# Stick-breaking attention on one core: the strict mask as an additive operand of the running product's scan

## The chip, the cores and the metric

The kernel runs on one core of a Trainium2 chip. The time is the device time of one execution in microseconds (us), taken as the median of several executions. The engines are TensorE (PE for matmuls, PEld for weight loads), VectorE (DVE), ScalarE (ACT), GpSimd (POOL) and SyncE (SP), which issues the DMAs.

## The reference, cut to what matters

Two layers, each a token mixer with two attention branches and a squared-ReLU MLP, over 1024 tokens of width 1024, in float32. The change touches the stick-breaking branch (8 heads of 64), of which this is the core:

```python
z = jnp.einsum('bqhd,bshd->bhqs', qb, kb).astype(jnp.float32) * scale
...
strict = s_idx < t_idx
log_keep = jnp.where(strict, -jax.nn.softplus(z), 0.0)
tail = lax.cumsum(log_keep, axis=3, reverse=True) - log_keep
w = jnp.where(strict, jnp.exp(jax.nn.log_sigmoid(z) + tail), 0.0)
outs.append(jnp.einsum('bhqs,bshd->bqhd', w.astype(v.dtype), vb))
```

In words: query t gives key s < t the weight sigmoid(z_ts) times the product of sigmoid(-z_tj) over all keys j between s and t, and no weight to keys s >= t.

## The kernel before

The whole program is one instruction stream per engine, written out by a planner at build time. Each piece of work is a Python generator (a process) that names the engine it wants and an estimated cost; the planner grants each engine to the waiting process of the lowest rank and emits its instructions in that order. On the chip each engine then runs its own list in order and waits where an operand is not there yet. So a changed cost or wait in one process can shift the order of others around it.

A layer has these stages: RMSNorm with transposes (L436), projections, sliding-window attention, stick-breaking attention (`sb_phase`), the merge of both branches under gates, the output projection, and the MLP. Float32 products are made of three matmuls on split operands (`three`, L346 to L348). The gate projections (`gates`, tiles `hT` and `wh` or `wl`, 512 columns wide) have the lowest priority and fill PE wherever a stage leaves it free; five of the sixteen gate blocks start late in `sb_phase` and end after it.

Inside `sb_phase`, each head is cut into four chunks `ci` of two query tiles `tt` (128 queries each). For a query tile the keys 0 to 128(tt+1) are taken in segments of at most 512 columns that start at `c0`: one segment for tt < 4, two (`c0` = 512, then `c0` = 0) for tt >= 4. That makes 12 segments for a head, and 192 for 8 heads and two layers. `weights` handles one of them:

- PE: two matmuls form the scores `z` (L979, L980). In the segment that holds the diagonal (c1 == n, 128 of the 192) a third matmul (L982) adds `sb_mask`, a bf16 tile that is 0 below the diagonal and -1e30 on and above it, with the bf16 identity `ident_b` as weights.
- ACT: `keep` = sigmoid(-z) (L988) and `cc` = sigmoid(z) (L991). The four `keep` tiles are 513 columns wide; column 512 holds 1.0.
- DVE: a scan over `keep[:, lo+1:513]` from right to left multiplies up the running product in place (L999, with `lo` = 512 - m for m columns). A lower segment (`c0` = 0 of two) starts its scan from `carry`, which the upper one made with one 128x1 multiplication (L1003). Then `cc` is multiplied by the products (L1006).
- POOL: a lower segment's column 512 is set back to 1.0 (L1009) and the `keep` tile is free.

Then `chunk` transposes the weights on PE (L1050, fp32, with the identity), ACT and DVE split them into `th` and `tl` (L1056, L1058), and PE multiplies them by the values `vall` (L1082, L1083). The result `o` (L1088, L1090) goes to the scratch `o_sb` (L1093), which the merge loads again (L322). `a_slots` (4) hands out the `keep` tiles, `c_slots` (7) the `cc` tiles, and `Bank("z")` four of the eight PSUM banks.

Of the kernel before, what the change touches and what calls it, by code (L numbers as in the profile page):

```python
# [9 lines left out]
F32 = mybir.dt.float32  # L10
F32R = mybir.dt.float32r
BF16 = mybir.dt.bfloat16
AF = mybir.ActivationFunctionType
ALU = mybir.AluOpType
AX = mybir.AxisListType

P = 128
T = 1024
D = 1024
# [5 lines left out]
NEG = -1e30  # L25
# [36 lines left out]
def f32(ap):  # L62
    return ap.bitcast(F32)
# [135 lines left out]
def tile_hybrid_trunk(ctx: ExitStack, tc: tile.TileContext, x, g_mix, g_mlp, g_rope, sinks, rope,  # L199
                      w_swa, w_qk, w_v, w_gate, w_br, w_out, w_up, w_down, out):  # L200
    nc = tc.nc
# [5 lines left out]
    def act_set(name):  # L207

        if tables_[0] != name:
            tables_[0] = name  # L210
            nc.scalar.preload_act_table_set(name)
# [4 lines left out]
    def pool(name, side="left", space=None):  # L216
        kw = {} if space is None else {"space": space}
        if space is None:
            kw["side"] = side
            kw["reuse_waits"] = "tile"  # L220
        return tc.alloc_tile_pool(name=name, bufs=1, **kw)
# [3 lines left out]
    cp = pool("const")  # L225
# [1 line left out]
    tp = pool("acts")  # L227
    gp = pool("stage")

    ident = cp.tile([P, P], F32, name="ident")  # L230
    make_identity(nc, ident)
    ident_r = cp.tile([P, P], F32R, name="ident_r")
    nc.vector.tensor_copy(ident_r, ident)
    ident_b = cp.tile([P, P], BF16, name="ident_b")
    nc.vector.tensor_copy(ident_b, ident)
    sb_mask = cp.tile([P, P], BF16, name="sb_mask")
    nc.gpsimd.memset(sb_mask, 0.0)
    nc.gpsimd.affine_select(out=sb_mask, in_=sb_mask, compare_op=ALU.is_gt, fill=NEG, base=0,
                            pattern=[[-1, P]], channel_multiplier=1)
    win_mask = cp.tile([P, 256], F32, name="win_mask")  # L240
    nc.gpsimd.memset(win_mask, 0.0)
    prev, cur = win_mask[:, 0:P], win_mask[:, P:256]
    nc.gpsimd.affine_select(out=prev, in_=prev, compare_op=ALU.is_gt, fill=-NEG, base=0,
                            pattern=[[1, P]], channel_multiplier=-1)
    nc.gpsimd.affine_select(out=cur, in_=cur, compare_op=ALU.is_ge, fill=-NEG, base=0,
                            pattern=[[-1, P]], channel_multiplier=1)
# [5 lines left out]
    def act(n):  # L252
        return n * .00083 + .095

    def dve(n):
        return n * .00104 + .068
# [4 lines left out]
    def scan(n):  # L261
        return n * .00225 + .04

    def mm(n):
        return max(n, 256) * .000417 + .0133
# [589 lines left out]


    def sb_phase(l, base, start, opened, q_opened, hT, o_scr, finished, late):
        sb, vall = None, None

        def open_pool():  # L860
            nonlocal sb, vall
            yield opened
            sb = pool("sb")
            vall = sb.tile([P, NT, SBH, 2, HD], F32R, name="vall")
            sb_pool[:] = [sb]
            for i in range(4):
                keeps.append(sb.tile([P, 513], F32, name=f"keep{i}"))
                nc.gpsimd.memset(keeps[i][:, 512:513], 1.0)
            ready.set(sb)

        ready = Event(plan)
        keeps = []
        plan.spawn(open_pool(), base)
        v_ev = [[Event(plan) for _ in range(NT)] for _ in range(2)]
        qk_ev = [Event(plan, 2) for _ in range(SBH)]
        qk_slots = Slots(plan, 2)
        a_slots, c_slots, t_slots, o_slots = Slots(plan, 4), Slots(plan, 7), Slots(plan, 3), Slots(plan, 2)
# [87 lines left out]
        def weights(h, tt, c0, carry_in, carry_out, z_done, got):  # L965
            n = P * (tt + 1)
            c1 = min(n, c0 + 512)
            m = c1 - c0
            yield ready
            yield qk_ev[h]  # L970
            qs, k1, k2 = qk_ev[h].value
            yield a_slots
            yield c_slots
            b = Bank("z")
            yield from b.take()
            yield "P", 2 * max(mm(m) if m > 128 else .11, .11) + (.06 if c1 == n else 0)
            z = b.tile()[:, :m]
            qt = qs[:, tt * P:(tt + 1) * P]
            nc.tensor.matmul(z, qt, k1[:, c0:c1], start=True, stop=False)  # L979
            nc.tensor.matmul(z, qt, k2[:, c0:c1], start=False, stop=c1 != n)  # L980
            if c1 == n:
                nc.tensor.matmul(z[:, m - P:m], ident_b, sb_mask, start=False, stop=True)  # L982
            z_done.done()

            keep, lo = keeps.pop(), 512 - m
            yield "A", act(m)
            act_set(SIGMOID)
            nc.scalar.activation(keep[:, lo:512], z, AF.Sigmoid, scale=-1.0)  # L988
            yield "A", act(m)
            cc = sb.tile([P, 512], F32, tag="c", name="c", bufs=7)[:, :m]  # L990
            nc.scalar.activation(cc, z, AF.Sigmoid)  # L991
            b.free()
            ini = 1.0
            if carry_in:
                yield carry_in
                ini = carry_in.value
            yield "D", scan(m)
            later = keep[:, lo + 1:513]
            nc.vector.tensor_tensor_scan(later[:, ::-1], later[:, ::-1], later[:, ::-1], ini, ALU.mult, ALU.bypass)  # L999
            if carry_out:  # L1000
                yield "D", .12
                carry = sb.tile([P, 1], F32, tag="carry", name="carry", bufs=6)
                nc.vector.tensor_tensor(carry, later[:, 0:1], keep[:, lo:lo + 1], ALU.mult)  # L1003
                carry_out.set(carry)
            yield "D", dve(m)
            nc.vector.tensor_tensor(cc, cc, later, ALU.mult)  # L1006
            if carry_in:
                yield "G", .1
                nc.gpsimd.memset(keep[:, 512:513], 1.0)  # L1009
            keeps.append(keep)  # L1010
            a_slots.release()
            got.set(cc)

        last_av = [None]
# [1 line left out]
        def chunk(h, ci, z_done):  # L1016
# [3 lines left out]
            for i, c0 in enumerate(starts):  # L1020
                for tt in (2 * ci, 2 * ci + 1):
                    got = Event(plan)
                    seg[tt, c0] = got
                    two = len(starts) == 2
                    got.carry = Event(plan) if two and c0 else None
                    cin = seg[tt, 512].carry if two and not c0 else None
                    plan.spawn(weights(h, tt, c0, cin, got.carry, z_done, got), rank + i * 2 + (tt % 2))
# [869 lines left out]
    def driver():  # L1897
# [4 lines left out]
        for l in range(depth):  # L1902
# [37 lines left out]
            plan.spawn(swap_right(swp, projected, q_opened), base)  # L1940
            swa_phase(l, base, sw, swp, hT, normed, o_swa, tab_scr, done, sb_on, projected)
            sb_phase(l, base, sb_on, opened, q_opened, hT, o_sb, sb_done, sb_late)
            yield done
            sw.release()
# [158 lines left out]
```

## Time and profile before

| | |
|---|---|
| median of 3 executions | 2726.43 us (2725.91 to 2731.25) |
| the profiled execution's own time | 2727.98 us |
| its span from the first instruction to the last | 2726.2 us |
| PE busy | 2691.2 us, 99% of the span |
| DVE, ACT, POOL busy | 1904.0, 1402.4, 8.9 us |
| mean granted TensorE clock | 0.996 of full speed |

The profile is of one execution, which lies 1.55 us above the median. A PE that is busy all the time isn't one at its fastest: matmuls overlap, so what one costs is read from the distance between its start and the start of the next, not from its duration.

### The profile page before, as it was taken

The page shows a single profiled execution, that of the slowest core. Times are in us where ns is not written, and L with a number is a line of the kernel's source. Part 1 is how long each engine was busy: PE and PEld are TensorE (multiplying, and loading weights), DVE is VectorE, ACT ScalarE, POOL GpSimd, SP SyncE. Part 2 cuts the span into 40 slices and gives each one's busy share as a digit, 9 for nine tenths or more (in the row PEclk, how much of TensorE's full clock was granted, in tenths as well). Part 3 has the DMA queues.
Part 4 walks back from the last instruction along what each step waited for, and adds up shares of the span by engine and source line. Part 5 has one row for each costly group of instructions (what it writes and reads, how often), then busy time and mean ns, then how long its engine had stood idle before and what let it go on. Part 6 is the DMA issues. An engine that isn't in the chain of part 4 may idle for free.

```text
span 2726.2 us, 37142 instructions
## 1 busy us (share of the span) xinstructions
PE 2691.2 (99%) x13568; PEld 2280.9 (84%) x13568; DVE 1904.0 (70%) x3269; ACT 1402.4 (51%) x2777; POOL 8.9 (0%) x83
## 2 busy tenths in 40 slices
PE   7999999999999999999999999999999999999999
PEld 7888888888878888888888988888888788888887
DVE  6665888855597777767766657887646877768664
ACT  5775556643365445333457766565424644553332
POOL 0000000000000000000000000000000000000000
PEclk9999999999999999999999999999999999999999
DMA  4222221164034447996433222123530444489972
GB/s 169 82 91 71 62 62 56 52 229 164 31 120 161 142 165 265 350 375 246 160 123 94 65 63 66 58 58 97 213 147 31 147 138 160 151 318 354 339 265 88
DMA packets 159382, 411.00 MB, mean 151 GB/s; under 512 B 18656, under 2 KB 32992, under 8 KB 159200
## 3 DMA queue, kind: packets, MB, share of 16 engines
q1 hardware_dynamic: 159200, 408.63, 42.9%
q8 instruction: 107, 1.75, 0.2%
q14 instruction: 75, 0.61, 0.1%
HBM read 285.88 MB, written 114.29 MB: 147 GB/s over the span
## 4 chain that ended last, share of the span: by engine, by line
PE 95%; DVE 2%; ACT 1%; DMA 1%; issue 0%; SPq 0%; DVEq 0%; ACTq 0%
PE bank L346 28%; PE bank L347 28%; PE bank L348 27%; PE bank L1050 2%; PE bank L1083 1%; PE bank L979 1%; PE bank L980 1%; PE bank L1082 1%; PE bank L694 1%; PE bank L436 1%; PE bank L761 1%; PE bank L784 0%; PE bank L783 0%; PE bank L668 0%; PE bank L982 0%
## 5 line engine op out<-in xcount | busy, mean ns | idle before, releaser
L1266 ACT CAST operand<-dr 128x1024 fp32r<-128x1024 f32 x224 | 220.3, 1048 | 348.8 <-PE bank L348 179.1
L347 PE MATMUL bank<-operand 128*128 128x512 f32 x896 | 348.8, 389 | 0.5 <-DVE operand L1269 0.5
L346 PE MATMUL bank<-operand 128*128 128x512 f32 x896 | 348.9, 389 | 0.0
L1269 DVE TENSOR_TENSOR operand<-dr,operand 128x1024 fp32r<-128x1024 f32 x224 | 262.7, 1222 | 123.3 <-ACT operand L1266 123.0
L348 PE MATMUL bank<-operand 128*128 128x512 f32 x896 | 348.6, 389 | 0.0
L346 PE MATMUL bank<-hT,wh 128*128 128x512 f32 (+1 forms) x776 | 312.3, 402 | 0.0
L348 PE MATMUL bank<-hT,wl 128*128 128x512 f32 (+1 forms) x776 | 302.8, 390 | 0.0
L347 PE MATMUL bank<-hT,wh 128*128 128x512 f32 (+1 forms) x776 | 302.4, 390 | 0.0
L347 PEld LDWEIGHTS bank<-operand 128*128 128x128 f32 x896 | 168.2, 188 | 36.2 <-DVE operand L1269 1.4
L348 PEld LDWEIGHTS bank<-operand 128*128 128x128 f32 x896 | 168.2, 188 | 34.9
L346 PEld LDWEIGHTS bank<-operand 128*128 128x128 f32 x896 | 168.2, 188 | 34.8
L1266 ACT CAST wh<-raw 128x512 fp32r<-128x512 f32 x128 | 78.6, 614 | 187.4 <-DVE raw L1280 127.3
L348 PEld LDWEIGHTS bank<-hT,wl 128*128 128x128 f32 x776 | 146.5, 189 | 31.6
L347 PEld LDWEIGHTS bank<-hT,wh 128*128 128x128 f32 x776 | 147.2, 190 | 23.7 <-DVE hT L395 0.2
L346 PEld LDWEIGHTS bank<-hT,wh 128*128 128x128 f32 x776 | 147.3, 190 | 23.3
L332 ACT CAST wh<-raw 128x1024 fp32r<-128x1024 f32 x88 | 92.4, 1051 | 102.6 <-PE bank L348 76.6
L335 DVE TENSOR_TENSOR wl<-raw,wh 128x1024 fp32r<-128x1024 f32 x88 | 107.1, 1219 | 53.4 <-ACT wh L332 52.5
L999 DVE TENSOR_TENSOR_SCAN keep<-keep 128x128 f32<-128x128 f32 (+3 forms) x128 | 100.1, 809 | 16.2 <-ACT keep L988 16.2
L988 ACT ACTIVATE keep<-bank 128x128 f32<-128x128 f32 (+1 forms) x192 | 91.3, 499 | 38.7 <-PE bank L982 23.1
L1058 DVE TENSOR_TENSOR tl<-bank,th 128x512 fp32r<-128x512 f32 (+1 forms) x160 | 97.5, 626 | 18.2 <-ACT th L1056 16.6
L1056 ACT CAST th<-bank 128x512 fp32r<-128x512 f32 (+1 forms) x160 | 83.3, 546 | 49.2 <-PE bank L1050 46.1
L1280 DVE TENSOR_TENSOR dr<-dr 128x1024 f32<-128x1024 f32 x64 | 78.1, 1224 | 40.7 <-DMA dr<-t_scr 16.2
(201 smaller groups left out, 6592.8 us busy)
## 6 DMA issues: line engine op xcount, KB each, us to landing
dr<-in_w_down_dram SPq DMA_DIRECT2D x144, 512.0 KB, 7.7
dr<-u_scr SPq DMA_DIRECT2D x112, 512.0 KB, 6.9
u_scr<-up SPq DMA_DIRECT2D x160, 256.0 KB, 2.8
raw<-in_w_up_dram SPq DMA_DIRECT2D x68, 512.0 KB, 3.5
raw<-in_w_gate_dram SPq DMA_DIRECT2D x32, 512.0 KB, 4.2
g_scr<-stage SPq DMA_DIRECT2D x64, 256.0 KB, 2.4
gate<-g_scr SPq DMA_DIRECT2D x64, 256.0 KB, 3.0
u_scr<-stage SPq DMA_DIRECT2D x64, 256.0 KB, 4.0
```

The lines of the kernel that those rows point to most:

```text
L332: nc.scalar.copy(hi[:, :n], raw[:, :n])
L335: nc.vector.tensor_tensor(lo[:, :n], raw[:, :n], f32(hi[:, :n]), ALU.subtract)
L346: nc.tensor.matmul(ps_ap, ah, bh, start=first, stop=False)
L347: nc.tensor.matmul(ps_ap, ah, bl, start=False, stop=False)
L348: nc.tensor.matmul(ps_ap, al, bh, start=False, stop=last)
L988: nc.scalar.activation(keep[:, lo:512], z, AF.Sigmoid, scale=-1.0)
L999: nc.vector.tensor_tensor_scan(later[:, ::-1], later[:, ::-1], later[:, ::-1], ini, ALU.mult, ALU.bypass)
L1056: nc.scalar.copy(th[:, :n], tr[:, :n])
L1058: nc.vector.tensor_tensor(tl[:, :n], tr[:, :n], f32(th[:, :n]), ALU.subtract)
L1266: nc.scalar.copy(op.hi(j, n), src)
L1269: nc.vector.tensor_tensor(op.lo(j, n), src, f32(op.hi(j, n)), ALU.subtract)
L1280: nc.vector.tensor_tensor(out, a, b, op)
```

## The change

The mask matmul, its bf16 identity and the mask tile go. The scan of a segment takes in column 512 too, so it runs over m + 1 columns from `keep[:, 512]` down to `keep[:, lo]`. For a segment with the diagonal its second operand is a new constant tile, `begins`: zero but for an identity in the columns 384 to 511. The scan now starts from 0 and computes state = keep * state + begins, so that the running product is 0 to the right of the diagonal, is set to 1 on it, and multiplies up from there. The product that `cc` takes in is that of the column to its right, so keys on and above the diagonal get weight 0. For a lower segment (`c0` = 0 of two) column 512 first gets the last product of the upper segment by a copy on DVE; this replaces both the `carry` multiplication and POOL's reset. The upper segment's `keep` tile is now held (`Shared`) until that copy has read it. The identity `ident` is now the fp32r tile `ident_r` seen as fp32, and `make_identity` works in the place of `win_mask`, which is written after it. The four `keep` tiles get their 1.0 from DVE instead of POOL, beside the filling of `begins`, when the phase's pool opens.

```diff
-    nc.vector.tensor_copy(ident_r, ident)
-    ident_b = cp.tile([P, P], BF16, name="ident_b")
-    nc.vector.tensor_copy(ident_b, ident)
-    sb_mask = cp.tile([P, P], BF16, name="sb_mask")
...
+    make_identity(nc, win_mask[:, 0:P])
     ident_r = cp.tile([P, P], F32R, name="ident_r")
...
+    nc.vector.tensor_copy(ident_r, win_mask[:, 0:P])
+    ident = f32(ident_r)
...
-                nc.gpsimd.memset(keeps[i][:, 512:513], 1.0)
+                nc.vector.memset(keeps[i][:, 512:513], 1.0)
+
+            begins = sb.tile([P, 513], F32, name="begins")
+            nc.vector.memset(begins, 0.0)
+            nc.vector.tensor_copy(begins[:, 384:512], ident)
...
-            yield "P", 2 * max(mm(m) if m > 128 else .11, .11) + (.06 if c1 == n else 0)
+            yield "P", 2 * max(mm(m) if m > 128 else .11, .11)
...
-            nc.tensor.matmul(z, qt, k2[:, c0:c1], start=False, stop=c1 != n)
-            if c1 == n:
-                nc.tensor.matmul(z[:, m - P:m], ident_b, sb_mask, start=False, stop=True)
+            nc.tensor.matmul(z, qt, k2[:, c0:c1], start=False, stop=True)
...
-            ini = 1.0
+
+            run = keep[:, lo:513][:, ::-1]
             if carry_in:
                 yield carry_in
-                ini = carry_in.value
-            yield "D", scan(m)
-            later = keep[:, lo + 1:513]
-            nc.vector.tensor_tensor_scan(later[:, ::-1], later[:, ::-1], later[:, ::-1], ini, ALU.mult, ALU.bypass)
+                first, other = carry_in.value
+                yield "D", .15
+                nc.vector.tensor_copy(keep[:, 512:513], first)
+                other.done()
+                yield "D", scan(m)
+                nc.vector.tensor_tensor_scan(run, run, run, 1.0, ALU.mult, ALU.bypass)
+            else:
+                yield "D", scan(m)
+                nc.vector.tensor_tensor_scan(run, run, begins[:, lo:513][:, ::-1], 0.0, ALU.mult, ALU.add)
+            use = Shared(2 if carry_out else 1, lambda: (keeps.append(keep), a_slots.release()))
             if carry_out:
-                yield "D", .12
-                carry = sb.tile([P, 1], F32, tag="carry", name="carry", bufs=6)
-                nc.vector.tensor_tensor(carry, later[:, 0:1], keep[:, lo:lo + 1], ALU.mult)
-                carry_out.set(carry)
+                carry_out.set((keep[:, lo:lo + 1], use))
             yield "D", dve(m)
-            nc.vector.tensor_tensor(cc, cc, later, ALU.mult)
-            if carry_in:
-                yield "G", .1
-                nc.gpsimd.memset(keep[:, 512:513], 1.0)
-            keeps.append(keep)
-            a_slots.release()
+            nc.vector.tensor_tensor(cc, cc, keep[:, lo + 1:513], ALU.mult)
+            use.done()
```

How the instructions stand is shown at three places. First PE, at the head of the stick-breaking stage of the first layer, where the first four score tiles of head 0 are made (`bank` is a PSUM tile, `hT` and `wh` or `wl` belong to the value projection). Before:

```order
L979 MATMUL bank<-k_3015,qs 128x128
L980 MATMUL bank<-k_3016,qs 128x128
L982 LDWEIGHTS ident_b
L982 MATMUL bank<-sb_mask,ident_b 128x128
L979 MATMUL bank<-k_3015,qs 128x256
L980 MATMUL bank<-k_3016,qs 128x256
L982 LDWEIGHTS ident_b
L982 MATMUL bank<-sb_mask,ident_b 128x128
L979 MATMUL bank<-k_3015,qs 128x384
```

and with the change (the same lines are L977 and L978 there):

```order
L977 MATMUL bank<-k_3010,qs 128x128
L978 MATMUL bank<-k_3011,qs 128x128
L977 MATMUL bank<-k_3010,qs 128x256
L978 MATMUL bank<-k_3011,qs 128x256
L977 MATMUL bank<-k_3010,qs 128x384
```

The mask and its weight load are gone between the score matmuls. Over the program that is 128 matmuls; of the masks of before, 115 have a three-pass or score or value matmul behind them, and 13 a group of transposes (L1050). Behind the last `vall` matmul of a layer's phase, 126 gate matmuls of 128x512 stood before the first matmul of the merge (`op`); now 108 stand there, since 18 have moved to places inside the phase. Outside the two stick-breaking phases the order on PE is the same.

Second DVE, at the first two lower segments of head 0 (a scan is named SCALAR_TENSOR_TENSOR here). Before:

```order
L1003 TENSOR_TENSOR carry<-keep_2993 128x1
L999 SCALAR_TENSOR_TENSOR keep_2995<-keep_2995 128x256
L1006 TENSOR_TENSOR c<-c,keep_2993 128x128
L1003 TENSOR_TENSOR carry<-keep_2995 128x1
L999 SCALAR_TENSOR_TENSOR keep_2989<-keep_2989,carry 128x512
```

and with the change:

```order
L1001 SCALAR_TENSOR_TENSOR keep_2987<-keep_2987,begins 128x257
L995 COPY keep_2981<-keep_2985 128x1
L1006 TENSOR_TENSOR c<-c,keep_2987 128x256
L1054 TENSOR_TENSOR tl<-bank,th 128x384
L1054 TENSOR_TENSOR tl<-bank,th 128x512
L909 TENSOR_TENSOR vall<-bank,vall 128x4x64
L998 SCALAR_TENSOR_TENSOR keep_2981<-keep_2981 128x513
```

The 128x1 multiplication behind the upper scan has become a 128x1 copy ahead of the lower one, 64 of each; 12 of the 64 copies stand right ahead of the scan that needs them, the others have work between. Third DVE again, where the phase's pool opens in the first layer, with the change:

```order
L786 TENSOR_TENSOR ob<-ob,bank 64x512
L862 MEMSET keep_2981 128x1
L862 MEMSET keep_2983 128x1
L862 MEMSET keep_2985 128x1
L862 MEMSET keep_2987 128x1
L865 MEMSET begins 128x513
L866 COPY begins<-ident_r 128x128
L909 TENSOR_TENSOR vall<-bank,vall 128x4x64
L948 TENSOR_TENSOR k_3011<-bank,k_3010 64x512
```

Six instructions have come between the last `ob` of the sliding-window attention and the first store of the values `vall`, which followed each other directly before.

## Rows read from the trace of the kernel before

**Rows 1.** The profile's page: span, and PE's busy time, share and instructions.
```profile
span 2726.2 us, 37142 instructions
PE 2691.2 (99%) x13568; PEld 2280.9 (84%) x13568; DVE 1904.0 (70%) x3269; ACT 1402.4 (51%) x2777; POOL 8.9 (0%) x83
```

**Rows 2.** Windows over the stick-breaking phases; busy us of PE, PEld, DVE, ACT, POOL, clock, DMA.
```profile
268.00:543.00 275.00, 275.00 (x1717) 239.62 (x1716) 232.15 (x391) 170.18 (x369) 3.15 (x32) 1.00 0.20 57
1620.00:1894.00 274.00, 274.00 (x1712) 238.58 (x1711) 231.89 (x391) 170.32 (x369) 3.15 (x32) 1.00 0.20 57
```

**Rows 3.** Waits of PE, first and last of eight: total us, times, longest.
```profile
PE bank L346 <- ACT t L1354: 12.4, 2, 6.2
...
PE bank L668 <- DVE a L616: 0.5, 1, 0.5
```

**Rows 4.** The mask's line: duration ns min/median/max, first and last start.
```profile
L982 PE MATMUL bank<-sb_mask,ident_b x128: 229/230/233, 269.0 to 1876.7; 128*128 128x128 bf16 x128
```

**Rows 5.** Timeline of PE from 268.8 us: start, duration, instruction.
```profile
268.86 0.22 PE L979 MATMUL bank<-k,qs 128*128 128x128 f32 x1
268.92 0.28 PE L980 MATMUL bank<-k,qs 128*128 128x128 f32 x1
269.04 0.23 PE L982 MATMUL bank<-sb_mask,ident_b 128*128 128x128 bf16 x1
269.08 0.36 PE L979 MATMUL bank<-k,qs 128*128 128x256 f32 x1
269.28 0.28 PE L980 MATMUL bank<-k,qs 128*128 128x256 f32 x1
269.40 0.23 PE L982 MATMUL bank<-sb_mask,ident_b 128*128 128x128 bf16 x1
...
272.21 0.23 PE L982 MATMUL bank<-sb_mask,ident_b 128*128 128x128 bf16 x1
272.28 0.50 PE L1050 MATMUL bank<-ident,c 128*128 128x128 f32 x3
```

**Rows 6.** Timeline of PE from 336.3 us, a mask with gate matmuls behind it.
```profile
336.34 0.23 PE L982 MATMUL bank<-sb_mask,ident_b 128*128 128x128 bf16 x1
336.38 0.47 PE L346 MATMUL bank<-hT,wh 128*128 128x512 f32 x1
336.69 0.39 PE L347 MATMUL bank<-hT,wh 128*128 128x512 f32 x1
336.92 0.40 PE L348 MATMUL bank<-hT,wl 128*128 128x512 f32 x1
```

**Rows 7.** Timeline of PE from 530.6 us, a segment without a mask, gate matmuls behind it.
```profile
530.61 0.39 PE L980 MATMUL bank<-k,qs 128*128 128x512 f32 x1
530.84 0.40 PE L346 MATMUL bank<-hT,wh 128*128 128x512 f32 x1
531.08 0.39 PE L347 MATMUL bank<-hT,wh 128*128 128x512 f32 x1
```

**Rows 8.** Groups of DVE, shapes apart: busy us, mean ns, idle before.
```profile
L999 DVE TENSOR_TENSOR_SCAN keep<-keep,carry 128x512 f32<-128x512 f32 x64 | 80.8, 1272 | 0.7 <-ACT keep L988 0.6
...
L999 DVE TENSOR_TENSOR_SCAN keep<-keep 128x512 f32<-128x512 f32 x32 | 38.4, 1199 | 0.0
...
L999 DVE TENSOR_TENSOR_SCAN keep<-keep 128x128 f32<-128x128 f32 x32 | 13.4, 418 | 16.2 <-ACT keep L988 16.2
...
L1003 DVE TENSOR_TENSOR carry<-keep 128x1 f32<-128x1 f32 x64 | 8.2, 147 | 0.1
```

**Rows 9.** Timeline from the start: two 128x1 DVE instructions, the second needing the first.
```profile
10.56 0.15 DVE L359 TENSOR_TENSOR rs_a<-y 128x1 f32<-128x1 f32 x1
10.75 0.16 DVE L361 TENSOR_TENSOR rs_a<-rs_a,v 128x1 f32<-128x1 f32 x1
```

**Rows 10.** Timeline of DVE where the first layer's stick-breaking pool opens.
```profile
253.14 0.69 DVE L950 TENSOR_TENSOR k<-bank,k 64x512 fp32r<-64x512 f32 x1 [5.12 <-ACT k L948]
```

**Rows 11.** Timeline of SP's DMA issues: the last `o_sb` store, and its first load.
```profile
543.22 0.45 SPq L1093 DMA_DIRECT2D o_sb<-o  x1
...
557.49 2.59 SPq L322 DMA_DIRECT2D raw<-o_sb  x3
```

More of the change, by code (lines that the diff above doesn't have):

```diff
@@ L228, in tile_hybrid_trunk @@
     gp = pool("stage")
-    ident = cp.tile([P, P], F32, name="ident")
-    make_identity(nc, ident)
+    win_mask = cp.tile([P, 256], F32, name="win_mask")
+    make_identity(nc, win_mask[:, 0:P])
     ident_r = cp.tile([P, P], F32R, name="ident_r")
-    nc.vector.tensor_copy(ident_r, ident)
-    ident_b = cp.tile([P, P], BF16, name="ident_b")
-    nc.vector.tensor_copy(ident_b, ident)
-    sb_mask = cp.tile([P, P], BF16, name="sb_mask")
[L237 to L240, printed above, removed]
+    nc.vector.tensor_copy(ident_r, win_mask[:, 0:P])
+    ident = f32(ident_r)
     nc.gpsimd.memset(win_mask, 0.0)
@@ L857, in sb_phase @@
     def sb_phase(l, base, start, opened, q_opened, hT, o_scr, finished, late):
-        sb, vall = None, None
+        sb, vall, begins = None, None, None
         def open_pool():
-            nonlocal sb, vall
+            nonlocal sb, vall, begins
             yield opened
```

## The prediction

> **What bounds the kernel now.** I began with the page: PE is busy for 2691 of 2726 us [rows 1], so the first question is whether any other engine can set the end where the change acts. The windows over the two stick-breaking phases (275 and 274 us) answer it: PE is busy for every microsecond of both, at the full granted clock, while DVE has 43 and 42 us without work, ACT more, and the DMA engines are used at 0.20 [rows 2]. Then the list of PE's waits: eight rows, from the 12.4 us at the start of an MLP down to 0.5 us in the sliding-window attention, and none at a score (L979, L980), mask (L982), transpose (L1050) or value matmul (L1082, L1083) [rows 3]. So in these phases no operand comes late to PE, and the phases last as long as PE's list of matmuls takes. What the change takes out of that list is worth what it occupies there, as long as the rest keeps up.
>
> **What a mask matmul occupies.** Its duration of 230 ns [rows 4] is no measure, since matmuls overlap; I read starts. The mask at 269.04 is followed at 269.08, so it holds PE for 0.04 us itself. But the matmul behind it holds PE longer than its kind does: the score matmul of 256 columns from 269.08 to 269.28, 0.20 us, where the next one of 256 columns takes 0.12 (269.28 to 269.40) [rows 5]. Behind the mask at 336.34 a gate matmul of 512 columns takes 0.31 us (336.38 to 336.69), where its neighbour takes 0.23 [rows 6]. Each time the follower loses 0.08 us. That this comes from the mask and not from the end of a score pair is seen at a segment that has no mask: there a gate matmul directly behind the score matmul takes 0.24 us (530.84 to 531.08) [rows 7]. So a mask costs 0.12 us, or by the rounding of starts to 0.01 us somewhere from 0.11 to 0.14; I take 0.125.
>
> **What is removed from PE.** Of the 128 masks [rows 4], 115 have such a follower: 115 x 0.125 = 14.4 us (12.7 to 16.1). The other 13 stand ahead of transposes, where I count only the mask's own hold, 0.07 us (272.21 to 272.28): 0.9 us [rows 5]. There may be a third part, ahead of the mask: the score matmul of 128 columns from 268.92 holds PE for 0.12 us until the mask, and its twin from 268.86 only 0.06 us [rows 5]. 32 of the masks close a segment of 128 columns, so this is 0 to 32 x 0.06 = 1.9 us; nothing shows what such a matmul holds without the mask behind it, and I take the middle, 1.0. The sum is 14.4 + 0.9 + 1.0 = 16.3 us (13.6 to 18.9).
>
> [...]
>
> **What DVE gets, and why I cost it at nothing.** All 192 scans get one column more: from 418 ns at 128 columns to 1199 at 512 [rows 8] a column is 2.03 ns, so 0.4 us in all. The 64 scans that start from a carry lose the pointer to it. Such a scan takes 1272 ns against 1199 without one [rows 8]; that is 64 x 0.073 = 4.7 us less. The 64 carry multiplications of 147 ns become 64 copies of the same shape. No copy of 128x1 is in the trace; I take 147 ns as well (bounds: nothing, and 0.19 us, the distance of two such instructions where the second needs the first [rows 9]). Where copy and scan stand directly together, 12 times, the scan starts up to 0.19 us behind: 2.3 us at most. So DVE's work changes by -4.7 + 0.4 and 0 to +2.3 us, which is somewhat less over both phases, in which it has 85 us free [rows 2]. The cover is thin only in stretches, so a late weight would show first as a wait of the transposes.
>
> The scan of the 128 diagonal segments now multiplies and adds, with a second tile as operand. No scan with an adding second step is in the trace; the bounds are no difference (before, too, two operands were named, both the same tile) and one more column's worth of half a scan, 1.0 ns, for each column, below as a rival. I take no difference.
>
> The opening of the pool puts six instructions into DVE's list ahead of the first `vall`. By the nearest kinds, four of 128x1 at 147 ns, one fill of 513 columns that can't well take longer than a scan of 512 (1199 ns), and a copy of 128 columns below a scan of 128 (418 ns) [rows 8], they are at most 2.2 us for a layer. Soon behind, DVE stands idle for 5.12 us until L950 [rows 10], which hides them; without that cover they would be 4.4 us for both layers. POOL's 64 resets go; nobody waited on them in the list for PE. At the program's start the transposes now need DVE's cast of `ident_r`; it stands in DVE's order ahead of `h`, which they need anyway, so this costs nothing.
>
> **What is held longer.** An upper `keep` tile is free only once the lower segment has copied its last product. With four tiles, the next chunk's first sigmoid on ACT can start later; behind it queue `cc`'s sigmoid, the `th` casts, and so the transposes on PE. The planner knows of this hold and has put gate matmuls ahead of those transposes: 18 of them, 18 x 0.23 = 4.1 us [rows 6], came into each phase from behind it. So a phase itself shrinks by 16.3/2 - 4.1 = 4 us, and the stretch behind it by the rest.
>
> There the next thing that could be late is the merge. It needs `o_sb`: the last store is issued at 543.22, the first load at 557.49 [rows 11]. Those 14 us were filled by gate matmuls; 4.1 less leaves 10, enough for a store to land. Everything behind stands in the old order and moves up.
>
> **The rivals.**
>
> *Part of it is given back* (chance 0.12). PE, now 0.125 us faster at each mask, reaches some transposes before the products are there. For it: DVE is at 84% over the phases [rows 2], and each chunk goes PE, ACT, DVE, PE. Against: PE had no such wait at all before [rows 3]. If each of the 64 chunks lost 0.1 to 0.2 us, 6 to 13 us would go: 2716 to 2723.
>
> *Only the mask's own hold comes back* (0.04). The 0.08 us would belong to the follower, whoever precedes it; 128 x 0.04 = 5.1 us gives 2721.3. Rows 7 speak against it. [...]
>
> *The phases become DVE's* (0.05). If the planner's new order, with `keep` tiles held longer, ties PE to DVE, the whole 16 us turns into waits: 2726, no change. Against it, again, 85 us of free DVE time.
>
> *The scan with an addition is slower* (0.04), the case on the other side. At 1.0 ns more a column and (128 + 256 + 384 + 512)/4 = 320 columns in the mean, 0.32 us a scan: 128 x 0.32 = 41 us on DVE. Felt in full, that is 2710.4 + 41 = 2751. It decides from (16 + 5.5)/128 = 0.17 us a scan, felt in full, since DVE's free time covers some. [...]
>
> **How the numbers follow.** The likeliest case (0.75) is the sum, with 0.3 us off for small waits: 16 us. The profiled execution took 2727.98 us in all, 2726.2 of it the span; 2727.98 - 16 = 2712.0. The median of the runs is 1.55 us lower, so I say 2710.4. That case by itself reaches from 2726.4 - 18.9 = 2707.5 to 2726.4 - 12 = 2714.4, the sum's bounds with up to 1.6 us of waits. The range goes up through most of the given-back case, to 2721, and down to 2707; what it leaves out is the DVE-bound and slow-scan cases and the tails. A change within 0.2% (5.5 us) is about what a measurement of this kernel can't tell from none. Faster: 0.75, nearly all of 0.12 and a bit of 0.04, 0.88. Same: the DVE-bound case and half of the own-hold one, 0.07. Slower: the slow scan and what a wrong order might do, 0.05.
>
> **What would show it.** In the profile after: 13,440 matmuls, busy PE in both phases without a wait at L1046 (the transposes), gate matmuls behind score pairs at 0.23 us, scans of 513 columns near 1.2 us with `begins` and without, copies near 0.15 us, and phases some 4 us shorter. Wrong I'd be if PE waits on DVE in those windows, if scans with `begins` are longer than the others, or if score pairs still delay their followers.

## The result and the profile after

The changed kernel takes 2712.19 us (median of 4 executions, 2710.46 to 2713.47), the kernel before 2727.14 (4 executions, 2725.91 to 2731.25). The medians differ by 15.0 us, or 0.55%. The ratio of the runs is 0.9939, a little lower than that of the medians (0.9945), with a 95% interval of 0.9927 to 0.9952. I had forecast 2710.4, from 2707 to 2721.

The page of the profiled execution (2710.46 us in all) answers to [rows 1]: 128 matmuls fewer, 18.5 us less of busy PE, a span 17.5 us shorter. POOL keeps 9 instructions of 83.

```profile
span 2708.7 us, 36685 instructions
PE 2672.7 (99%) x13440; PEld 2276.0 (84%) x13440; DVE 1903.1 (70%) x3280; ACT 1400.8 (52%) x2777; POOL 2.6 (0%) x9
```

The windows answer to [rows 2]. They are 270 us long where those of before were 275 and 274, since the phases end sooner, and PE is still busy in every microsecond, at the full clock; DVE has 40 us free in each.

```profile
268.00:538.00 270.00, 270.00 (x1659) 240.56 (x1659) 230.11 (x389) 168.58 (x368) 0.00 (x0) 1.00 0.21 59
1610.00:1880.00 270.00, 270.00 (x1662) 240.68 (x1661) 230.52 (x390) 169.33 (x368) 0.00 (x0) 1.00 0.21 59
```

The list of PE's waits has eight rows, as in [rows 3] (here the first two and the last: total us, times, longest): none is at a score (L977, L978), a transpose (L1046) or a value matmul of the phases. No wait took the place of the masks.

```profile
PE bank L430 <- DVE h L419: 13.9, 5, 10.6
PE bank L340 <- ACT t L1350: 12.4, 2, 6.2
...
PE bank L430 <- DVE v L415: 0.2, 1, 0.2
```

Two pieces of PE's timeline answer to [rows 5] and [rows 6]. In the first a gate matmul stands directly behind a score pair, and holds PE for 0.23 us (317.38 to 317.61) where it held it for 0.31 behind a mask. The second has a pair of 128 columns, with no mask behind it: its second matmul still holds PE for 0.11 us (337.03 to 337.14). A third piece shows an exception: directly behind a pair of 128 columns a gate matmul holds PE for 0.28 us (341.93 to 342.21), though no mask stands there. All four gate matmuls in such a place do, where the 14 behind pairs of 256 columns hold it for 0.23. That some score pairs still delay what follows them was one of my signs of being wrong; it bears on the size, below.

```profile
316.98 0.28 PE L978 MATMUL bank<-k,qs 128*128 128x128 f32 x1
317.09 0.33 PE L977 MATMUL bank<-k,qs 128*128 128x256 f32 x1
317.26 0.28 PE L978 MATMUL bank<-k,qs 128*128 128x256 f32 x1
317.38 0.39 PE L340 MATMUL bank<-hT,wh 128*128 128x512 f32 x1
317.61 0.39 PE L341 MATMUL bank<-hT,wh 128*128 128x512 f32 x1
...
336.97 0.22 PE L977 MATMUL bank<-k,qs 128*128 128x128 f32 x1
337.03 0.27 PE L978 MATMUL bank<-k,qs 128*128 128x128 f32 x1
337.14 0.33 PE L977 MATMUL bank<-k,qs 128*128 128x256 f32 x1
...
341.82 0.27 PE L978 MATMUL bank<-k,qs 128*128 128x128 f32 x1
341.93 0.45 PE L340 MATMUL bank<-hT,wh 128*128 128x512 f32 x1
342.21 0.39 PE L341 MATMUL bank<-hT,wh 128*128 128x512 f32 x1
```

DVE's groups, shapes apart, answer to [rows 8]: the scans with `begins` last no longer than those without it, and the copies (L995) take 137 ns where the multiplications took 147.

```profile
L998 DVE TENSOR_TENSOR_SCAN keep<-keep 128x513 f32<-128x513 f32 x64 | 77.5, 1217 | 1.0 <-ACT keep L984 0.5
L1001 DVE TENSOR_TENSOR_SCAN keep<-keep,begins 128x513 f32<-128x513 f32 x32 | 38.5, 1204 | 0.0
...
L995 DVE COPY keep<-keep 128x1 f32<-128x1 f32 x64 | 8.1, 137 | 0.0
```

**Where the 17.5 us of the two spans lie.** I take a phase from the start of its first score matmul to the start of the first merge matmul (`op`). Before, the two phases lasted 301.9 and 301.2 us, after 294.65 and 293.98: 14.5 us less. Of the other 3.0, 0.9 lie ahead of the first score matmul (268.86 before, 267.95 after) and 1.9 between the two phases, where the order on PE is the same as before. In the runs of this study the way to the first score matmul differed by up to 3.9 us between kernels that share it (257.1 to 261.1 us from the first matmul), so I don't count these as the change's. For the 1.9 us the granted clock gives most of a reason. At the start of the first layer's MLP PE waits for 6.2 us; within this wait the granted clock falls to 0.50 of full speed, and some time behind it returns to 1.00. In windows of 2 us it reads 0.64 from 766 us, 0.50 from 768, 0.80 from 776 and 1.00 from 778 before, and 0.74 from 758, 0.50 from 760, 0.55 from 764 and 1.00 from 766 after. Two windows of 30 us at this point (before, then after) have the same busy time of PE, but a mean granted clock of 0.83 and 0.89:

```profile
760.00:790.00 30.00, 23.44 (x94) 18.57 (x93) 28.56 (x48) 21.93 (x41) 0.00 (x0) 0.83 0.20 71
752.00:782.00 30.00, 23.44 (x99) 18.72 (x98) 29.86 (x51) 23.00 (x43) 0.00 (x0) 0.89 0.24 79
```

The difference is worth 30 x 0.06 = 1.8 us, an estimate from these two shares. I don't count it as the change's: mask_twice below, which has the most masks of all, has 0.89 there too. Nor is the clock all that differs between executions, for mask_f32r, at 0.89, has 1050.1 us between the phases, where the kernel before has 1049.8 and the changed one 1047.9. The medians differ by 15.0, close to what the phases lost.

### The profile page after: what moved, and what is told of

It is laid out like the page before. It is cut to its first block, busy times and chain, and to the rows that moved or that the text cites. A ratio compares the mean times of both kernels' runs of the same rounds, so it can differ in the third digit from the quotient of the medians.

```text
span 2708.7 us, 36685 instructions
## 1 busy us (share of the span) xinstructions
PE 2672.7 (99%) x13440; PEld 2276.0 (84%) x13440; DVE 1903.1 (70%) x3280; ACT 1400.8 (52%) x2777; POOL 2.6 (0%) x9
## 4 chain that ended last, share of the span: by engine, by line
PE 95%; DVE 2%; ACT 1%; DMA 1%; issue 0%; SPq 0%; DVEq 0%; ACTq 0%
PE bank L340 28%; PE bank L342 27%; PE bank L341 27%; PE bank L1046 2%; PE bank L1079 1%; PE bank L977 1%; PE bank L978 1%; PE bank L1078 1%; PE bank L688 1%; PE bank L755 1%; PE bank L430 1%; PE bank L778 1%; DMA raw<-in_w_gate_dram 0%; PE bank L777 0%; PE bank L662 0%
## 5 line engine op out<-in xcount | busy, mean ns | idle before, releaser
L1001 DVE TENSOR_TENSOR_SCAN keep<-keep,begins 128x129 f32<-128x129 f32 (+3 forms) x128 | 100.0, 811 | 10.0 <-ACT keep L984 9.8
L1580 DVE TENSOR_TENSOR stage<-bank,stage 128x512 f32<-128x512 f32 x96 | 66.0, 688 | 53.2 <-PE bank L342 53.2
```

Source lines behind the costliest of these rows:

```text
L1001: nc.vector.tensor_tensor_scan(run, run, begins[:, lo:513][:, ::-1], 0.0, ALU.mult, ALU.add)
L1580: nc.vector.tensor_tensor(out, a, b, ALU.add)
```

## The experiments

Each was timed beside the kernel before: the second time given is that kernel's median there, and the ratio is to it. The sum of the two phases, as defined above, is the sharper measure, read from the one profiled execution of each kernel: 603.2 us before, 588.6 after.

**mask_off: the kernel before without its mask matmul, nothing else.** Order, scan, carry and POOL's resets stay; the strict mask is left out of the result.

```diff
-            nc.tensor.matmul(z, qt, k2[:, c0:c1], start=False, stop=c1 != n)
-            if c1 == n:
-                nc.tensor.matmul(z[:, m - P:m], ident_b, sb_mask, start=False, stop=True)
+            nc.tensor.matmul(z, qt, k2[:, c0:c1], start=False, stop=True)
```

> The kernel before without its mask matmul and with nothing else changed: the planner's costs, and so the order, are those of before, and scan, carry, reset and holds of the keep tiles stay. It leaves the strict mask out. Theory (the mask's place in PE's list is the whole effect): each mask gives back its hold and its follower's loss, and the time falls as far as the changed kernel's did, 14 to 16 us below before, with the follower back at 0.23 us for 512 columns. Rival (the gain is from the scan without a carry pointer, the lost POOL reset or the new order): at most a third of it, 0 to 5 us. Rival (only the hold of 0.04 us): 5 us.

Measured: 2712.47 against 2728.07, 0.9943 (0.9930 to 0.9955), phases 588.9. That is the whole effect. The scan, the copies, the longer hold of `keep` and the moved gate matmuls together are worth 0.3 us of the phases. Since the order is that of before here, the starts can be summed by kind over both phases: the masks held PE for 5.43 us, the score matmuls lose 4.33, the gate matmuls 3.33, the 256-column value projections 0.79, the value matmuls 0.44, and the transposes gain 0.06. So 5.4 us are the masks' own. Of the other 8.8, 8.2 lie in the matmuls directly behind a mask, and 0.6 in the score matmuls directly ahead of one.

**mask_back: the changed kernel with a matmul of the mask's kind on zeros behind each of the 128 diagonal score pairs.** Its bf16 operands are zeros out of `begins`.

```diff
-            nc.tensor.matmul(z, qt, k2[:, c0:c1], start=False, stop=True)
+            nc.tensor.matmul(z, qt, k2[:, c0:c1], start=False, stop=c1 != n)
+            if c1 == n:
+                none_w, none = begins[:, 0:64].bitcast(BF16), begins[:, 64:128].bitcast(BF16)
+                nc.tensor.matmul(z[:, m - P:m], none_w, none, start=False, stop=True)
```

> The changed kernel with a bf16 matmul of 128x128 put back behind the score pair of every diagonal segment, on zeros, so it adds nothing; the planner isn't told, so the order is the changed kernel's. Theory: the time goes back to that of before, within 3 us, by 0.04 us a mask and 0.07 to 0.08 us a follower, and the scans with the second tile stay as fast. Rival (other parts of the change carry the gain): it stays 9 to 15 us below before.

Measured: 2728.17 against 2728.07, 0.9998 (0.9989 to 1.0006), phases 603.5: everything is gone again. PE's timeline of this kernel shows the loss return:

```profile
319.21 0.23 PE L981 MATMUL bank<-begins 128*128 128x128 bf16 x1
319.25 0.48 PE L340 MATMUL bank<-hT,wh 128*128 128x512 f32 x1
319.56 0.40 PE L341 MATMUL bank<-hT,wh 128*128 128x512 f32 x1
```

The timeline of its weight loads (PEld) at the same place:

```profile
319.20 0.10 PEld L981 LDWEIGHTS <-begins 128*128 128x128 bf16 x1
319.21 0.20 PEld L340 LDWEIGHTS bank<-hT,wh 128*128 128x128 f32 x1
```

The gate matmul holds PE for 0.31 us again. Its weights begin to load at 319.21, when the short matmul starts, and are in at 319.41, 0.16 us after the gate matmul's recorded start. In the changed kernel the same load starts with the 256-column score matmul and is in at 317.45, 0.07 us after the start at 317.38 (timeline of PEld, changed kernel):

```profile
317.26 0.19 PEld L340 LDWEIGHTS bank<-hT,wh 128*128 128x128 f32 x1
```

That suggests a reason: in these records a load starts with the matmul ahead of its own and takes 0.19 to 0.20 us, and a matmul that holds PE for 0.04 us is too short to cover it. The matmul of 128 columns needn't be a mask: the 0.28 us behind a pair of 128 columns, in the result, fit this too. The next three runs ask whether it is rather the type, the columns, or a price of every such matmul.

**mask_twice: the kernel before with the mask matmul issued twice** (the second adds -1e30 once more to scores that have it already).

```diff
             if c1 == n:
+                nc.tensor.matmul(z[:, m - P:m], ident_b, sb_mask, start=False, stop=False)
                 nc.tensor.matmul(z[:, m - P:m], ident_b, sb_mask, start=False, stop=True)
```

> The kernel before with the mask matmul issued twice. It tells whether the cost is one for each matmul or one for each switch to a bf16 matmul and back. If each costs the same: 14 to 16 us above before, 2741. If the loss of the follower is paid once for a run of bf16 matmuls: only the second's own hold is added, 0.04 to 0.06 us x 128, 5 to 8 us, 2733.

Measured: 2735.21 against 2728.07, 1.0024 (1.0015 to 1.0033), phases 610.1, 7.0 more than before: 55 ns for each added mask, half of what the first costs. PE's timeline:

```profile
336.52 0.28 PE L980 MATMUL bank<-k,qs 128*128 128x256 f32 x1
336.65 0.23 PE L982 MATMUL bank<-sb_mask,ident_b 128*128 128x128 bf16 x1
336.71 0.22 PE L983 MATMUL bank<-sb_mask,ident_b 128*128 128x128 bf16 x1
336.74 0.47 PE L346 MATMUL bank<-hT,wh 128*128 128x512 f32 x1
337.06 0.39 PE L347 MATMUL bank<-hT,wh 128*128 128x512 f32 x1
```

The gate matmul behind both holds PE for 0.32 us, as behind one. So its loss comes once for the two short matmuls, not with each of them.

**mask_f32r: the mask and its identity in fp32r instead of bf16.** Then no type changes between the score matmul, the mask and its follower.

```diff
-    sb_mask = cp.tile([P, P], BF16, name="sb_mask")
+    sb_mask = cp.tile([P, P], F32R, name="sb_mask")
...
-                nc.tensor.matmul(z[:, m - P:m], ident_b, sb_mask, start=False, stop=True)
+                nc.tensor.matmul(z[:, m - P:m], ident_r, sb_mask, start=False, stop=True)
```

> The kernel before with mask and identity in fp32r, the type of the matmuls around it, in place of bf16. If the follower's loss comes from the change of type: it goes, the mask itself then holds PE for 0.06 us like a score matmul of 128 columns, or 0.11, and the time falls by 1 to 8 us. If it comes from one more weight load that the short matmul can't cover: the follower still loses, or the mask holds PE longer, the cost of a mask stays at 0.11 to 0.13 us and the time within 3 us of before.

Measured: 2727.67 against 2728.07, 0.9996 (0.9987 to 1.0005), phases 602.9. PE's timeline:

```profile
338.16 0.22 PE L981 MATMUL bank<-sb_mask,ident_r 128*128 128x128 f32 x1
338.22 0.44 PE L345 MATMUL bank<-hT,wh 128*128 128x512 f32 x1
338.50 0.39 PE L346 MATMUL bank<-hT,wh 128*128 128x512 f32 x1
```

Over all 45 masks with a gate matmul behind them, the mask now holds PE for 0.07 us and its follower for 0.28, 0.05 more than its kind: 0.12 together, as with bf16, only split in another way. A change of type is not the cause.

**mask_wide: mask_back with 256 columns instead of 128** in the 96 segments that have them.

```diff
-                none_w, none = begins[:, 0:64].bitcast(BF16), begins[:, 64:128].bitcast(BF16)
-                nc.tensor.matmul(z[:, m - P:m], none_w, none, start=False, stop=True)
+                w = min(m, 2 * P)
+                none_w, none = begins[:, 0:64].bitcast(BF16), begins[:, 64:64 + w // 2].bitcast(BF16)
+                nc.tensor.matmul(z[:, m - w:m], none_w, none, start=False, stop=True)
```

> The changed kernel with the put-back bf16 matmul on zeros, 256 columns wide in place of 128 wherever the segment has them (96 of 128). If a mask's price is the time of one more weight load, which a matmul of 128 columns is too short to cover, then twice the columns cost no more: the mask holds PE longer and its follower loses less, and the time is within 2 us of the narrow one's, 2728. If columns are paid on top of a fixed price: 128 x 96 columns at the 0.44 ns a column of the score matmuls, 5 us more, 2733.

Measured: 2729.71 against 2728.01, 1.0005 (0.9996 to 1.0014), phases 603.4, the same as with 128 columns. PE's timeline, with a value projection of 256 columns behind the wide matmul:

```profile
271.10 0.29 PE L982 MATMUL bank<-begins 128*128 128x256 bf16 x1
271.14 0.36 PE L340 MATMUL bank<-wh,hT 128*128 128x256 f32 x1
271.34 0.28 PE L341 MATMUL bank<-wl,hT 128*128 128x256 f32 x1
271.45 0.28 PE L342 MATMUL bank<-wh,hT 128*128 128x256 f32 x1
```

Hold 0.04 and follower 0.20 instead of 0.12, as with the narrow one; that the mask itself would hold PE longer, as I had expected, isn't seen. The second half of the columns is free: for a mask of 128 columns, what is paid doesn't go by its columns. (The price of 0.12 us is also what a score matmul of 256 columns holds PE for, 317.26 to 317.38 in the changed kernel, so a mask of 256 costs no more than such a score matmul.) The equal price agrees with a follower that waits for its own weights, loading since the short matmul's start: here from 271.10 to 271.30 in PEld's timeline, 0.16 us past the follower's start, as in mask_back.

**slow_scan: the changed kernel with one more DVE instruction behind each of the 128 diagonal scans** (`cc` = max(`cc`, `cc`), mean 0.46 us), unknown to the planner, so that the order stays. It puts a price on the rival of a slow scan, and asks how much DVE work the phases can hide.

```diff
                 nc.vector.tensor_tensor_scan(run, run, begins[:, lo:513][:, ::-1], 0.0, ALU.mult, ALU.add)
+                nc.vector.tensor_tensor(cc, cc, cc, ALU.max)
```

> The changed kernel with one more DVE instruction behind each of the 128 scans that use the second tile: the maximum of the sigmoid tile with itself, over the segment's columns, which changes no value. By the multiplications of the same shapes it costs 0.2 to 0.6 us each, about 43 us over both phases, what a scan slower by 1 ns a column would cost; the planner isn't told. Theory: DVE has 40 us free in each phase, so most is covered, but some transposes had their products less than half a microsecond early; PE waits at them and 4 to 15 us are lost against the changed kernel. Rival (DVE is nowhere near the bound): less than 2 us. Rival (the phases follow DVE): 35 us or more.

Measured: 2746.07 against 2728.01, 1.0066 (1.0053 to 1.0078); phases 621.7, 33.0 more than the changed kernel's. My expectation failed: of 59 us of added DVE work (128 x 0.46) more than half was felt, though the windows show DVE with 33 us free in a stretch of 282:

```profile
268.00:550.00 282.00, 274.84 (x1643) 238.01 (x1642) 248.88 (x447) 168.60 (x367) 0.00 (x0) 1.00 0.19 55
```

Its list of PE's waits names the new one, at the value matmuls of `tl`, but gives it 13.2 us only:

```profile
PE bank L430 <- DVE h L419: 15.5, 6, 10.7
PE bank L1080 <- DVE tl L1055: 13.2, 28, 0.8
...
PE bank L1047 <- DVE c L1007: 0.5, 2, 0.2
```

The rest is hidden in its timeline of PE, of which two pairs of value matmuls are shown:

```profile
497.60 0.28 PE L1079 MATMUL bank<-th,vall 128*128 128x256 f32 x1
497.72 0.28 PE L1080 MATMUL bank<-tl,vall 128*128 128x256 f32 x1
...
499.69 0.28 PE L1079 MATMUL bank<-th,vall 128*128 128x256 f32 x1
500.04 0.38 PE L1080 MATMUL bank<-tl,vall 128*128 128x256 f32 x1
```

DVE's timeline ahead of the second pair says why:

```profile
498.85 0.67 DVE L1002 TENSOR_TENSOR c<-c 128x512 f32<-128x512 f32 x1
499.43 0.55 DVE L1055 TENSOR_TENSOR tl<-bank,th 128x384 fp32r<-128x384 f32 x1
```

From `th` to `tl` PE normally moves on after 0.12 us; here it takes 0.35, since `tl` is ready only at 499.98, behind the added instruction. It lost 0.23 us, but the matmul of 499.69 is drawn until 499.97, so all but 0.07 of them count as busy. By starts, 20.5 of the 33 us lie between a `th` and a `tl` value matmul, 8.3 between a `tl` and the next `th`, and 3.8 between two transposes.

**slow_scan_told: the same instruction, with its cost told to the planner**, which then orders the work by it.

```diff
+                yield "D", dve(m)
                 nc.vector.tensor_tensor(cc, cc, cc, ALU.max)
```

> The same as the kernel with the extra maximum behind each of the 128 scans, but the planner is told of its cost, so it writes the order of all engines for it. The untold one lost 34 us, mostly as PE waits for the low halves of the transposed weights. Theory (DVE has time enough in the phases, but an order in which PE has its operands half a microsecond early can't use it): told, gate matmuls stand where PE would wait and most of the loss goes, 2712 to 2722. Rival (the phases are bound by DVE's amount of work at that point): it stays above 2735.

Measured: 2724.88 against 2727.29, 0.9989 (0.9980 to 0.9998), a little above what I expected. The phases take 594.3, 5.6 more than the changed kernel's where slow_scan lost 33.0. The medians differ from the changed kernel's by 12.7, so some 7 us come elsewhere, mostly at the merge: the stretch between the two phases, which begins with it, is 6.8 us longer (1054.7 against 1047.9). There the list of PE's waits has rows that the changed kernel doesn't:

```profile
PE bank L342 <- DVE wl L329: 1.9, 3, 0.7
PE bank L340 <- ACT op L326: 1.4, 1, 1.4
PE bank L341 <- DVE op L329: 1.2, 2, 0.8
```

and the window behind the first merge matmul shows 2.7 us without PE work at a granted clock of 0.89; the 31 us from the same point of the changed kernel had no idle time and the clock at 1.00.

```profile
569.00:600.00 31.00, 28.32 (x111) 21.99 (x110) 19.52 (x23) 16.70 (x23) 0.00 (x0) 0.89 0.66 243
```

So DVE's free time hid nearly all of this work in an order that knows of it (5.6 us felt of 59), and less than half in one that doesn't (33.0 felt).

## Why the prediction was right

**The bound.** In these phases PE's list of matmuls sets the end, and what leaves the list leaves the time. This held: no wait appeared, mask_off alone gives the whole effect, and mask_back alone takes it away.

**The price of a mask.** I had taken 0.125 us where a long matmul follows; the phases lost 14.5/128 = 0.113 us a mask over all of them. mask_off gives the terms one by one:
- The masks' own hold was met: 5.43 us, where 115 x 0.04 + 0.9 = 5.5 was taken.
- The followers were taken too large: 115 x 0.085 = 9.8 us, where 8.3 came back. Behind 90 masks a follower got back 0.083 us, as forecast. Behind the other 25, which close a segment of 128 columns, it got back 0.032 only, because a score matmul of 128 columns delays its follower too, without a mask. One of the two places from which I read the 0.08 was such a place: the score matmul of 269.08 in [rows 5] holds PE for 0.20 us, and I compared it with 0.12, but behind a pair of 128 columns its kind takes 0.17 in the changed kernel (317.09 to 317.26). [rows 7], my check on score pairs without a mask, has a pair of 512 columns. With the own hold the 115 masks gave 12.9 us, just within my 12.7 to 16.1.
- The third part, the score matmul ahead of the mask: 1.0 us taken, within 0 to 1.9. It is 0.6, but spread over segments of all widths. In those of 128 columns, for which I had taken it, it is 0.1: the second matmul of such a pair holds PE for 0.11 us without any mask behind it.
- The 0.3 us that I took off for small waits weren't needed. Instead of 16.0 the phases lost 14.5, and the forecast is 1.8 us below the median; 0.7 of these lie in its start from a median before of 2726.43, where four executions give 2727.14.

**The rest of the order.** The gate matmuls moved as planned: a phase's stretch from its first score to its last value matmul shrank by 3.2 us in each layer (4 predicted), and the one behind it by 4.1 (4.1 predicted). What the merge loads from `o_sb` had 10.2 us left after the last store, where I had said 10, and an `o_sb` store landed 1.9 us after its issue (the median in the DMA issues of both kernels); SP's timeline answers to [rows 11]:

```profile
539.14 0.45 SPq L1089 DMA_DIRECT2D o_sb<-o  x1
...
549.30 2.59 SPq L316 DMA_DIRECT2D raw<-o_sb  x3
```

**DVE at nothing.** The scans that lost their carry's pointer went from 1272 to 1217 ns, 64 x 0.055 = 3.5 us less (4.7 predicted); the addition cost 1204 against 1199 for a scan one column shorter, so nothing. The opening of the pool is hidden by the same idle time as in [rows 10], now 4.27 us:

```profile
252.23 0.69 DVE L948 TENSOR_TENSOR k<-bank,k 64x512 fp32r<-64x512 f32 x1 [4.27 <-ACT k L946]
```

**The rivals.** Only the mask's own hold: refuted by mask_off and mask_back, which move 14 us where 5.1 was its price. Part given back, and phases that become DVE's: neither is seen, since PE waits for nothing there. The slow scan didn't occur. Its working said that DVE's free time would cover some of it. slow_scan puts a number on that, and it is less than I thought: in an order that didn't know of the work more than half came through, and 0.46 us a scan cost 33 us.

**What stays open.** Why the follower loses. In the records a follower's load starts with the matmul just ahead, or 0.05 us later behind a pair of 128 columns; it takes 0.19 to 0.20 us, and a short matmul doesn't cover that. In the changed kernel the weights of the gate matmul of 341.93 are in at 342.06 (timeline of PEld):

```profile
341.87 0.19 PEld L340 LDWEIGHTS bank<-hT,wh 128*128 128x128 f32 x1
```

The gate matmuls of these runs line up by when their weights are in, counted from their own recorded start: 0.07 us after it behind a pair of 256 columns, and they hold PE for 0.23; 0.13 us behind a pair of 128 columns or a mask in fp32r, and 0.28; 0.16 us behind any bf16 mask, single, second or wide, and 0.31 to 0.32. Weights that come 0.03 us later make the hold 0.03 us longer, so the loss fits a follower that waits for its own weights, with and without a mask. But no run shortened or took away this load alone, so it is argued from the records and not shown. A mask of 512 columns wasn't tried.

## What to carry to other kernels

Read what a short matmul costs from the starts of it and of the one behind it, against the same follower elsewhere: its own hold was a third of its price. Look also at what stands ahead of it: where a short matmul would still be left there, less comes back (0.03 us in place of 0.08 here). In a stage where PE never waited, the matmuls taken out were worth this price, whatever the other engines gained or lost, since no wait appeared. An engine's idle share says how much work could be hidden and not how much will be: where a fixed order wasn't made for the added work, DVE with 33 us free in 282 let more than half of it through.

## What the runs showed of the hardware that I had not expected

In these kernels a bf16 matmul behind an fp32r one of 256 or more columns cost 0.12 us (0.04 and 0.08 in its follower) with 128 and with 256 columns of its own alike, and 0.12 in fp32r, but a second one directly behind it only 0.055. A gate matmul behind an fp32r matmul of 128 columns lost 0.05 us even without it (0.28 against 0.23). The list of waits understated those of PE: the record of a value matmul of 256 columns lasts 0.28 us where the next starts 0.12 behind it, so that up to 0.16 us of each wait count as busy (13.7 us listed of 33 lost in slow_scan). And a scan that adds a second tile lasted as long as one that doesn't (1204 against 1199 ns), while one that starts from a pointer was 0.07 us longer ([rows 8]); 0.055 of these went when the same scans started from a constant (1217 ns).
